# A decoder step on one core: operands and split weights of the matmuls placed at multiples of 128 bytes, moving rows and next weight rows at other parity

## The chip, the cores and the metric

The kernel runs on 1 core of one Trainium2 chip. The metric is the device time of one execution in microseconds; less is better. Engines are named as in the profile: PE is TensorE (its weight loads are listed apart as PEld), DVE is VectorE, ACT is ScalarE, POOL is GpSimd, SP is SyncE, which issues most DMA transfers.

## The reference: what is computed

One decoder layer for two sets of tokens: 512 prompt tokens and 8 x 8 sample tokens, 576 columns in all, with model width 1024. Every sub-layer is preceded by an RMS norm whose gain and shift come from a conditioning vector.

```python
x = x + 0.5 * g1 * swiglu(modulate(rms_norm(x, n1_g), sh1, sc1), w1_gate, w1_up, w1_down)
z = modulate(rms_norm(x, nm_g), sh2, sc2) @ w_in        # u, v, q, k, rv, rg, ga, gb
o_a = gelu(u) * chunk_spatial_mix(layer_norm(gelu(v)))
o_b = head_rms(retention(rotary(q), rotary(k), rv, S0)) * silu(rg)
x = x + g2 * ((sigmoid(ga) * (o_a @ w_a) + sigmoid(gb) * (o_b @ w_b)) @ w_o)
x = x + 0.5 * g3 * swiglu(modulate(rms_norm(x, n2_g), sh3, sc3), w2_gate, w2_up, w2_down)
y = rms_norm(x, final_g)
```

The feed-forward width is 2816; there are 8 retention heads. Everything is float32. Outputs are the tokens, the retention states and the normalised v rows of the samples.

## The kernel before, in words

**Split operands.** A float32 value is written as a high part, rounded to TensorE's one-pass float32 format (`F32R`), and a low part, the rest. A product of two such values takes three matmuls: high weights by high operand, high weights by low operand, low weights by high operand. ScalarE writes the high part (a copy that converts), VectorE the low part (a subtraction). Each matmul loads its own 128x128 block of weights, so the order on TensorE is load, matmul, load, matmul, and each load runs beside the matmul before it.

**Where the matmuls are.** `prod` (L648) multiplies 288 columns, half of the 576 tokens, with four blocks of 128 contraction rows, and serves both gate and up projections of the two FFNs and most of the input projection. Its moving operands are the tiles that `op` makes, filled by `Operands.hi` and `Operands.lo` (L561, L563, L568, L572 and near), and its weights come from class `Weights`: `put_hi` (L666) and `put_lo` (L674, L676). The classes `Plain` and `Pair` built on it combine four quarter products with sums of operands and of weights, so that seven products do the work of eight. `proj` (L482) multiplies 320 or 256 columns and serves the down and output projections; its weights come through `Down` and `load_w`, its moving operands are high and low tiles of 576 columns. L1350, L1363 and L1580 compute values with the roles turned: the weight matrix moves, in 256 columns, and the token tile is the stationary side. L1504 and L1515 are small products of the retention core.

**Where the tiles lie.** Tiles are rows of bytes in each of the 128 partitions. `set_in` makes a tile for split weights and starts them `INTO` = 28 elements, 112 bytes, into it. In the built program these weights start at 240, some at 112, past a multiple of 256 bytes. A moving tile of `prod` holds high parts in `[:, 0]` and low parts in `[:, 1]`, each four blocks of 288 columns; a block is 1152 bytes, nine times 128, so that blocks start in turn at 128 and at 0 past a multiple of 256. The moving tiles of `proj` start at 128 past such a multiple.

**What sets the order.** Within the three stretches `BEGIN`, `INTO_MIX` and `INTO_FFN2` a written list of steps sets the order on every engine; elsewhere it is the order of the code, with side work (conditioning products, operand splits of the mixer) put in by `tick` after each product at estimated times. Weights are fetched by SyncE's DMA queue into a ring of raw tiles, split, and used.

Of the kernel before, what the change touches and what calls it, by code (L numbers as in the profile page):

```python
# [8 lines left out]
F32 = mybir.dt.float32  # L9
F32R = mybir.dt.float32r  # L10
AF = mybir.ActivationFunctionType
ALU = mybir.AluOpType
# [3 lines left out]
P = 128  # L16
# [7 lines left out]
H = T // 2  # L24
# [10 lines left out]
FSLOT = 12  # L35
GROUPS = (5, 6, 5, 6)

INTO = 28
HALF = (slice(0, H), slice(H, T))
PART = (slice(0, 320), slice(320, T))  # L40
PW = (320, T - 320)
# [42 lines left out]
def layer_kernel(ctx: ExitStack, tc: tile.TileContext, a):  # L84
    nc = tc.nc
    PE, DVE, ACT, POOL = nc.tensor, nc.vector, nc.scalar, nc.gpsimd
# [5 lines left out]
    wp = ctx.enter_context(tc.tile_pool(name="wp", bufs=1))  # L92
# [40 lines left out]
    def nine(home, shape, dt=F32R):  # L133
        return now[home].tile(shape, dt, tag="x", name=nm(home), bufs=4 if home == "xa" else 3)

    def nine_w(shape):

        return set_in(now["xs1"], shape, 9 * 256 - shape[1] * shape[2] * shape[3], tag="x", name=nm("xw"), bufs=3)
# [4 lines left out]
    def bank():  # L143
        return pp.tile([P, 512], F32, tag="ps", name=nm("ps"), bufs=8)

    def set_in(home, shape, room=INTO, **kw):

        n = 1
        for d in shape[1:]:
            n *= d  # L150
        t = home.tile([P, n + room], F32R, **kw)[:, INTO:INTO + n]
        if len(shape) == 4:
            return t.rearrange("p (a b c) -> p a b c", b=shape[2], c=shape[3])
        return t.rearrange("p (a b c d) -> p a b c d", b=shape[2], c=shape[3], d=shape[4])
# [9 lines left out]
    def whl(shape):  # L164
        small = len(shape) == 3 and shape[1] == 1
        tag = "whs" if small else "whl"
        return set_in(
            now["whs"] if small else wp, [P] + shape, INTO if small else 64, tag=tag, name=nm(tag), bufs=1 if small else 4
        )

    def load_raw(src, k0, kc, c0, cols):
        raw = raw4([kc, cols])
        nc.sync.dma_start(
            out=raw, in_=src[k0 * P:(k0 + kc) * P, c0:c0 + cols].rearrange("(k p) c -> p k c", p=P)
        )
        return raw

    def high_low(shape):
        t = whl([2] + shape)
        return t[:, 0], t[:, 1]  # L180
# [331 lines left out]
    ops = {}  # L512

    def op(name):
        if name not in ops:
            t = nine("xs1" if name in ops["near"] else "xa", [P, 2, 4, H])
            ops[name] = t[:, 0], t[:, 1]
        return ops[name]

    class Operands:  # L520
# [20 lines left out]
        def s(self, p):  # L541
            c0, c1 = 2 * p, 2 * p + 2
            u4 = self.hb[:, c0:c1, NP:T].rearrange("p c (b l) -> p c b l", l=LS)
            s0 = self.sh * 8
            for m, op in ((self.g[:, c0:c1, 1:9], ALU.mult), (mT[:, s0 + c0:s0 + c1, 1:9], ALU.add)):
                DVE.tensor_tensor(out=u4, in0=u4, in1=m.unsqueeze(3).broadcast_to([P, 2, NB, LS]), op=op)

        def blocks(self, j):
            hb = self.hb
            return tuple(hb[:, c:c + 2, cl] for c in (2 * j, 4 + 2 * j) for cl in HALF)  # L550
# [7 lines left out]
        def hi(self, name, j):  # L558
            hi, src = op(name)[0][:, 2 * j:2 * j + 2], self.src(name, j)
            if name == "N11":  # L560
                ACT.activation(out=hi, in_=src, func=AF.Copy, scale=-1.0)  # L561
            else:
                ACT.copy(out=hi, in_=src)  # L563

        def lo(self, name, j):
            (hi, lo), src = (t[:, 2 * j:2 * j + 2] for t in op(name)), self.src(name, j)
            if name == "N11":
                DVE.scalar_tensor_tensor(  # L568
                    out=lo, in0=src, scalar=-1.0, in1=hi.bitcast(F32), op0=ALU.mult, op1=ALU.subtract
                )  # L570
            else:
                DVE.tensor_tensor(out=lo, in0=src, in1=hi.bitcast(F32), op=ALU.subtract)  # L572
# [86 lines left out]

    class Weights:  # L660
        def put_hi(self, names, src, neg=False):
            hl = whl([2, len(names), 512])
            if neg:
                ACT.activation(out=hl[:, 0], in_=src, func=AF.Copy, scale=-1.0)
            else:
                ACT.copy(out=hl[:, 0], in_=src)  # L666
            self.hl[names] = hl, src, neg

        def put_lo(self, names):
            hl, src, neg = self.hl[names]  # L670
            if neg:
                now["lo"] = DVE.scalar_tensor_tensor(
                    out=hl[:, 1], in0=src, scalar=-1.0, in1=hl[:, 0].bitcast(F32), op0=ALU.mult, op1=ALU.subtract
                )  # L674
            else:
                now["lo"] = DVE.tensor_tensor(out=hl[:, 1], in0=src, in1=hl[:, 0].bitcast(F32), op=ALU.subtract)  # L676
            for i, m in enumerate(names):
                self.w[m] = (hl[:, 0, i], hl[:, 1, i])

        def block_of(self, dst, i, z):  # L680

# [280 lines left out]
    def home_wd(c, shape):  # L962
        return set_in(now["hl"], shape, 64, tag="wd", name=nm("wd"), bufs=2)

    def home_whl(c, shape):
        return home_wd(c, shape) if c in (0, 1, 4, 5) else whl(shape[1:])
# [122 lines left out]
    for c in range(KC):  # L1089
# [11 lines left out]
        out=xall[:, :, NP:T], in_=psS[:, 0:KC * NS].rearrange("p (c t) -> p c t", c=KC))  # L1101
# [631 lines left out]
    for i in range(2):  # L1733
        for n in range(NT):
            m, z = P if n < 4 else NS, NT * i + n
# [73 lines left out]
    def home_o(c, shape):  # L1809
        if c < 2:  # L1810
            return whl(shape[1:])
        if c < 5:
            return nine_w(shape)
        return home_wd(c, shape) if c < 7 else set_in(hb_pool, shape, tag="wo", name=nm("wo"), bufs=1)

    Wo = Down(a["w_o"][0], 0, KC, home_o)
    late = []

# [6 lines left out]
    for pr in ([0], [1], [2], [3], [4], [5], [6, 7]):  # L1825
# [41 lines left out]
    hb_pool = pool(greg, "hb", "right")  # L1867
# [184 lines left out]
```

## Time and profile before

| what | value |
|---|---|
| time, 3 runs | median 1672.13 us (1667.75 to 1672.86) |
| profiled execution | 1670.48 us, its span 1668.7 us |
| TensorE matmul | busy 1637.5 us, 98% of the span, 12548 instructions |
| VectorE | busy 1154.8 us, 69% |
| ScalarE | busy 784.0 us, 47% |
| GpSimd | busy 291.5 us, 17% |
| HBM traffic | 207.01 MB read, 43.02 MB written |
| granted TensorE clock, mean | 0.996 |

A row of the page's groups reads: line, engine, operation, written tile <- read tiles, shape, count | busy us, mean ns of one | idle time ahead of it and what ended it. Matmuls are pipelined: the duration of one (some 290 ns) is longer than the distance of two starts (some 130 ns), so the pace of TensorE is read from starts, or from the chain of waits, which gives the time and the count of an unbroken run.

### The profile page before, as it was taken

Reading aid. Unit: us, or ns where it says so; the run is one execution under the profiler, and the core shown is the slowest. Engines: PE = TensorE matmul, PEld = TensorE weight load, DVE = VectorE, ACT = ScalarE, POOL = GpSimd, SP = SyncE. Lnnn points to the kernel's source line nnn. Section 1 sums busy time; section 2 is a strip of 40 time slices with the busy share of each in tenths; the row PEclk is TensorE's granted clock in tenths of the full one; section 3 lists DMA queues with packets and bytes.
Section 4 is the critical chain, followed back from the end, with each engine's and each line's share of the span. In section 5 each row is a group of like instructions: output and inputs, shape, how many; then the busy total and the mean of one; then the engine's idle time right before and its main releaser. Section 6 shows DMA issues by size and latency. Waiting matters only on the chain. (4 is left out here: it accounts for less than half of the span.)

```text
span 1668.7 us, 31368 instructions
## 1 busy us (share of the span) xinstructions
PE 1637.5 (98%) x12548; PEld 1575.7 (94%) x12548; DVE 1154.8 (69%) x1835; ACT 784.0 (47%) x1331; POOL 291.5 (17%) x372
## 2 busy tenths in 40 slices
PE   7999999999999999999999999999999999999997
PEld 4899999999999999999999999998999999999997
DVE  6867857576696877755688554677748768576773
ACT  5634524344564556644445444443237435243454
POOL 0000000000411011113346343454131000000002
PEclk9999999999999999999999999999999999999999
DMA  9553444332537776764457474798540233332321
GB/s 303 145 153 103 140 138 129 114 102 86 177 119 210 220 219 192 222 199 166 149 176 256 156 192 148 209 257 267 163 135 17 82 92 98 92 90 85 96 86 58
DMA packets 300212, 252.09 MB, mean 151 GB/s; under 512 B 13593, under 2 KB 260633, under 8 KB 300066
## 3 DMA queue, kind: packets, MB, share of 16 engines
q1 hardware_dynamic: 284594, 206.76, 41.1%
q0 software_dynamic: 13168, 40.97, 8.8%
q10 hardware_dynamic: 2304, 2.36, 0.4%
q8 instruction: 98, 1.61, 0.4%
q14 instruction: 48, 0.39, 0.1%
HBM read 207.01 MB, written 43.02 MB: 150 GB/s over the span
## 5 line engine op out<-in xcount | busy, mean ns | idle before, releaser
L648 PE MATMUL ps<-xa,whl 128*128 128x288 f32 x3000 | 423.7, 296 | 5.5 <-ACT xa L561 2.1
L648 PEld LDWEIGHTS ps<-xa,whl 128*128 128x128 f32 x3000 | 404.7, 190 | 18.2 <-issue 4.2
L648 PE MATMUL ps<-xs,whl 128*128 128x288 f32 x2040 | 289.1, 295 | 0.8 <-ACT sn L657 0.6
L648 PEld LDWEIGHTS ps<-xs,whl 128*128 128x128 f32 x2040 | 274.0, 189 | 10.9 <-issue 4.2
L676 DVE TENSOR_TENSOR whl<-wraw,whl 128x1024 fp32r<-128x1024 f32 x192 | 234.5, 1223 | 54.2 <-ACT whl L666 48.3
L666 ACT CAST whl<-wraw 128x1024 fp32r<-128x1024 f32 x192 | 200.0, 1047 | 105.8 <-DVE wraw L790 64.6
L482 PEld LDWEIGHTS ps<-c,wd 128*128 128x128 f32 x1824 | 244.2, 189 | 3.5 <-issue 3.4
L482 PE MATMUL ps<-c,wd 128*128 128x320 f32 (+1 forms) x1824 | 247.4, 296 | 0.0
L482 PE MATMUL ps<-c,whl 128*128 128x256 f32 (+1 forms) x1368 | 191.8, 298 | 1.1 <-ACT c L192 0.7
L482 PEld LDWEIGHTS ps<-c,whl 128*128 128x128 f32 x1368 | 184.3, 189 | 3.1 <-DVE c L193 0.9
L469 POOL TENSOR_TENSOR x<-x,s 128x64 f32<-128x64 f32 x72 | 35.6, 495 | 808.6 <-DVE s L468 780.7
L463 DVE SCALAR_TENSOR_TENSOR x<-ps,gate,x 128x320 f32<-128x320 f32 (+1 forms) x128 | 61.1, 481 | 120.3 <-PE ps L482 120.3
L657 ACT COPY sn<-ps 128x288 f32<-128x288 f32 x195 | 77.4, 399 | 107.5 <-PE ps L648 107.0
L185 DVE TENSOR_TENSOR whl<-wraw,whl 128x1024 fp32r<-128x1024 f32 x56 | 77.9, 1393 | 67.4 <-ACT whl L184 67.1
L949 ACT CAST wd<-wraw 128x640 fp32r<-128x640 f32 (+2 forms) x58 | 45.3, 781 | 107.7 <-PE ps L482 98.3
L1350 PE MATMUL ps<-whl,xx 128*128 128x256 f32 x768 | 88.6, 275 | 0.0
L1350 PEld LDWEIGHTS ps<-whl,xx 128*128 128x128 f32 x768 | 87.8, 188 | 0.0
L648 PE MATMUL ps<-xs,whs 128*128 128x288 f32 x480 | 69.9, 294 | 0.0
L184 ACT CAST whl<-wraw 128x1024 fp32r<-128x1024 f32 x56 | 58.5, 1048 | 22.6 <-PE ps L482 14.5
L648 PEld LDWEIGHTS ps<-xs,whs 128*128 128x128 f32 x480 | 65.7, 189 | 0.0
L666 ACT CAST whs<-wraw 128x512 fp32r<-128x512 f32 x62 | 38.5, 621 | 55.7 <-PE ps L648 46.7
L954 DVE TENSOR_TENSOR wd<-wraw,wd 128x640 fp32r<-128x640 f32 (+2 forms) x58 | 53.4, 920 | 10.1 <-ACT wd L949 9.8
(285 smaller groups left out, 2223.1 us busy)
## 6 DMA issues: line engine op xcount, KB each, us to landing
ada<-in_w_ada_dram SPq DMA_DIRECT2D x56, 512.0 KB
wraw<-in_w_in_dram SPq DMA_DIRECT2D x96, 256.0 KB
wraw<-in_w_gate_dram SPq DMA_DIRECT2D x88, 256.0 KB
wraw<-in_w_up_dram SPq DMA_DIRECT2D x88, 256.0 KB
wraw<-in_w_in_dram SPq DMA_DIRECT2D x32, 512.0 KB
wraw<-in_w_down_dram SPq DMA_DIRECT2D x32, 384.0 KB
wraw<-in_w_down_dram SPq DMA_DIRECT2D x32, 320.0 KB
accd<-c POOLq DMA_DIRECT2D x32, 288.0 KB, 5.7
```

What stands on the lines that cost most here:

```text
L184: ACT.copy(out=hi, in_=raw)
L185: now["lo"] = (eng or DVE).tensor_tensor(out=lo, in0=raw, in1=hi.bitcast(F32), op=ALU.subtract)
L463: DVE.scalar_tensor_tensor(out=x[:, o:o + w], in0=ps[:, :w], scalar=g[:, c, 0:1], in1=x[:, o:o + w], op0=ALU.mult, op1=ALU.add)
L469: return lambda: POOL.tensor_tensor(out=x[:, NP:T], in0=x[:, NP:T], in1=u, op=ALU.add)
L482: PE.matmul(ps[:, :PW[h]], lhsT=s[:, k, c0:c0 + P], rhs=m[:, PART[h]], start=k == 0 and z == 0, stop=k == kc - 1 and z == 2,)
L648: PE.matmul(ps[:, :H], lhsT=s[:, j * P:(j + 1) * P], rhs=m[:, j, :], start=fresh and j == 0 and z == 0, stop=j == 3 and z == 2, skip_group ...
L657: ACT.copy(out=t, in_=ps[:, :H])
L666: ACT.copy(out=hl[:, 0], in_=src)
L676: now["lo"] = DVE.tensor_tensor(out=hl[:, 1], in0=src, in1=hl[:, 0].bitcast(F32), op=ALU.subtract)
L949: ACT.copy(out=hl[:, 0], in_=self.raw[c])
L954: DVE.tensor_tensor(out=lo, in0=self.raw[c], in1=hi.bitcast(F32), op=ALU.subtract)
L1350: PE.matmul(ps[:, :DV], lhsT=s, rhs=m, start=i == 0, stop=i == 23)
```

## The change

All split weights and moving operands start at multiples of 128 bytes (`LINE` = 32 elements). In `Weights` the high and the low block of a weight tile are no longer adjoining: the low block starts one `LINE` further, so that the two start at other parity when addresses are counted in rows of 128 bytes; `blocks` makes such a pair. In the moving tiles of `prod` the high and low parts of one contraction block adjoin (`[P, 4, 2, H]`, low first), where before all high parts came first. So while a high operand moves, the weights that load next start in a row of the other parity, and likewise for a low operand. `home_o`'s last tile starts at its tile's beginning. No instruction is added or removed; the high and low splits write two runs of 288 columns per instruction instead of one of 576.

```diff
-INTO = 28
+LINE = 32
...
-    def set_in(home, shape, room=INTO, **kw):
+    def set_in(home, shape, room=LINE, at=LINE, **kw):
...
-        t = home.tile([P, n + room], F32R, **kw)[:, INTO:INTO + n]
+        t = home.tile([P, n + room], F32R, **kw)[:, at:at + n]
...
+    def blocks(m):
+
+        if m == 1:
+            t = now["whs"].tile([P, 2 * 512 + 2 * LINE], F32R, tag="whs", name=nm("whs"), bufs=1)[:, LINE:]
+        else:
+            t = wp.tile([P, 2 * m * 512 + 2 * LINE], F32R, tag="whl", name=nm("whl"), bufs=4)
+        return (t[:, o:o + m * 512].rearrange("p (m c) -> p m c", m=m) for o in (0, m * 512 + LINE))
...
-            t = nine("xs1" if name in ops["near"] else "xa", [P, 2, 4, H])
-            ops[name] = t[:, 0], t[:, 1]
+            t = nine("xs1" if name in ops["near"] else "xa", [P, 4, 2, H])
+            ops[name] = t[:, :, 1], t[:, :, 0]
...
         def put_hi(self, names, src, neg=False):
-            hl = whl([2, len(names), 512])
+            hi, lo = blocks(len(names))
...
-            for i, m in enumerate(names):
-                self.w[m] = (hl[:, 0, i], hl[:, 1, i])
+                self.w[m] = hi[:, i], lo[:, i]
...
-        return home_wd(c, shape) if c < 7 else set_in(hb_pool, shape, tag="wo", name=nm("wo"), bufs=1)
+        return home_wd(c, shape) if c < 7 else set_in(hb_pool, shape, at=0, tag="wo", name=nm("wo"), bufs=1)
```

More of the change, by code (lines that the diff above doesn't have):

```diff
@@ L167, in whl @@
         return set_in(
-            now["whs"] if small else wp, [P] + shape, INTO if small else 64, tag=tag, name=nm(tag), bufs=1 if small else 4
+            now["whs"] if small else wp, [P] + shape, LINE if small else 64, tag=tag, name=nm(tag), bufs=1 if small else 4
         )
+    def blocks(m):
[4 more added lines that the diff above has]
+        return (t[:, o:o + m * 512].rearrange("p (m c) -> p m c", m=m) for o in (0, m * 512 + LINE))
     def load_raw(src, k0, kc, c0, cols):
@@ L661, in put_hi @@
         def put_hi(self, names, src, neg=False):
-            hl = whl([2, len(names), 512])
+            hi, lo = blocks(len(names))
             if neg:
-                ACT.activation(out=hl[:, 0], in_=src, func=AF.Copy, scale=-1.0)
+                ACT.activation(out=hi, in_=src, func=AF.Copy, scale=-1.0)
             else:
-                ACT.copy(out=hl[:, 0], in_=src)
-            self.hl[names] = hl, src, neg
+                ACT.copy(out=hi, in_=src)
+            self.hl[names] = hi, lo, src, neg
         def put_lo(self, names):
-            hl, src, neg = self.hl[names]
+            hi, lo, src, neg = self.hl[names]
             if neg:
                 now["lo"] = DVE.scalar_tensor_tensor(
-                    out=hl[:, 1], in0=src, scalar=-1.0, in1=hl[:, 0].bitcast(F32), op0=ALU.mult, op1=ALU.subtract
+                    out=lo, in0=src, scalar=-1.0, in1=hi.bitcast(F32), op0=ALU.mult, op1=ALU.subtract
                 )
             else:
-                now["lo"] = DVE.tensor_tensor(out=hl[:, 1], in0=src, in1=hl[:, 0].bitcast(F32), op=ALU.subtract)
+                now["lo"] = DVE.tensor_tensor(out=lo, in0=src, in1=hi.bitcast(F32), op=ALU.subtract)
             for i, m in enumerate(names):
-                self.w[m] = (hl[:, 0, i], hl[:, 1, i])
+                self.w[m] = hi[:, i], lo[:, i]
         def block_of(self, dst, i, z):
```

## The prediction

> **What bounds the kernel now.** I read the busy times first, then the chain of work that ended last, then the groups of matmuls by form, then single stretches of TensorE's timeline. The two head lines of the page:
>
> ```profile
> span 1668.7 us, 31368 instructions
> PE 1637.5 (98%) x12548; PEld 1575.7 (94%) x12548; DVE 1154.8 (69%) x1835; ACT 784.0 (47%) x1331; POOL 291.5 (17%) x372
> ```
>
> TensorE works for 98% of the span and VectorE, the next, for 69%. So the time is the number of matmuls times their spacing, and what matters is whether that spacing can move. The chain (start, length, what) gives it over long unbroken runs of the two lines that issue most matmuls, L648 (the FFN and input projections) and L482 (the down and output projections):
>
> ```profile
> 1330.73 31.94 PE ps L482 x240
> 1362.67 40.99 PE ps L648 x312
> 1429.38 38.37 PE ps L482 x288
> 1467.74 29.96 PE ps L648 x228
> ```
>
> 40.99 us / 312 = 131.4 ns for a 288-column matmul of L648, and 29.96 / 228 = 131.4 again. 38.37 / 288 = 133.2 for L482, whose matmuls are half 320 and half 256 columns wide. Nothing but TensorE is in those runs. The timeline of TensorE splits the widths, and has two other lines with the same 256 columns (start, length, line, names, shape; the length of a row runs past the next start, since matmuls are pipelined, so I divide the distance of two starts by the count):
>
> ```profile
> 784.49 5.75 PE L1580 MATMUL ps<-whl,xx 128*128 128x256 f32 x48
> 790.08 0.69 PE L1504 MATMUL ps<-c,onesr 128*128 128x288 f32 x4
> ...
> 796.15 11.04 PE L1350 MATMUL ps<-whl,xx 128*128 128x256 f32 x96
> 807.03 1.98 PE L1363 MATMUL ps<-whl,hs 128*128 128x256 f32 x16
> ...
> 989.82 1.12 PE L1515 MATMUL ps<-c,c 128*128 128x256 f32 x8
> 990.78 4.79 PE L482 MATMUL ps<-c,whl 128*128 128x256 f32 x36
> ...
> 1245.39 3.67 PE L482 MATMUL ps<-xa,wo 128*128 128x320 f32 x24
> 1248.90 3.03 PE L482 MATMUL ps<-xa,xw 128*128 128x256 f32 x24
> 1251.77 0.65 PE L441 MATMUL ps<-all,onesr 128*128 128x288 f32 x2
> ```
>
> L1350: (807.03 - 796.15) / 96 = 113.3 ns. L1515: 0.96 / 8 = 120.0. L482 at 256 columns: 2.87 / 24 = 119.6, at 320 columns 3.51 / 24 = 146.3. All three load new 128x128 weights for each matmul and none waits, yet L1350 is 6 to 7 ns faster on the same shape. The widths of L482 give the price of a column, (146.3 - 119.6) / 64 = 0.417 ns, so L1350's spacing carried to the other widths is 113.3 + 32 x 0.417 = 126.7 ns at 288 and 140.0 at 320. L648 stands 4.7 ns above that, L482 6.3 at each width. The groups by form say the same in durations:
>
> ```profile
> L648 PE MATMUL ps<-xa,whl 128*128 128x288 f32 x3000 | 423.7, 296 | 5.5 <-ACT xa L561 2.1 <-ACT whl L666 1.4 <-DVE whl L676 1.3
> L482 PE MATMUL ps<-c,wd 128*128 128x320 f32 x912 | 143.8, 310 | 0.0
> L482 PE MATMUL ps<-c,wd 128*128 128x256 f32 x912 | 118.9, 283 | 0.0
> L1350 PE MATMUL ps<-whl,xx 128*128 128x256 f32 x768 | 88.6, 275 | 0.0
> L1515 PE MATMUL ps<-c,c 128*128 128x256 f32 x64 | 9.2, 282 | 0.0
> ```
>
> 275 ns in L1350 against 283 in L482 at one width.
>
> **What differs between the fast and the slow lines.** Only where the operands lie. Take the byte distance, modulo 256, from the start of a moving operand to the start of the weights that load beside it (the next matmul's), as the built program places them. L1350, L1363 and L1580: 144, the weights starting on a multiple of 128. L1515: 0, both on multiples of 128. L482: 112, the weights 16 bytes short of such a multiple. L648: 112 or 240, changing with every contraction block, since a block's columns are nine rows of 128 bytes. So 144 costs 113.3 ns; 0 and 112 cost about 120; 112 and 240 in turn cost 131.4 where 126.7 would match. In the changed program the distance is 128 on 5,727 of 5,744 successive pairs of L648, 3,966 of 3,987 of L482, and all of L1350; that the edit fails to do what it says is no rival.
>
> **The change, part by part.** It adds and removes no instruction, and the order on all five engines is row for row the same.
>
> *Spacing of L648.* The distance becomes 128, which the trace never holds for a stretch. Bounds: from the row at 144 (126.7 ns) to the row at 0, 120.0 + 32 x 0.417 = 133.3. I take 126.7. Parity alone does not part fast from slow (112 is other parity for most of the bytes and slow), alignment of the weights alone does not either (0 is aligned and slow); 144 has both, and 128 has both. There are 3000 + 2040 + 480 + 264 = 5784 such matmuls by their groups:
>
> ```profile
> L648 PE MATMUL ps<-xs,whl 128*128 128x288 f32 x2040 | 289.1, 295 | 0.8 <-ACT sn L657 0.6
> L648 PE MATMUL ps<-xs,whs 128*128 128x288 f32 x480 | 69.9, 294 | 0.0
> L648 PE MATMUL ps<-xa,whs 128*128 128x288 f32 x264 | 38.8, 295 | 0.0
> ```
>
> 5784 x 4.7 = 27.2 us saved; by the other bound 5784 x 1.9 = 11.0 lost.
>
> *Spacing of L482.* The groups of the line, with shortest, median and longest duration in ns:
>
> ```profile
> L482 PE MATMUL ps<-c,wd x1824: 277/307/495, 110.5 to 1651.5; 128*128 128x320 f32 x100, 128*128 128x256 f32 x83
> L482 PE MATMUL ps<-c,whl x1368: 276/306/500, 417.8 to 1657.7; 128*128 128x320 f32 x98, 128*128 128x256 f32 x98
> L482 PE MATMUL ps<-xx,whl x384: 276/307/500, 909.4 to 1044.7; 128*128 128x320 f32 x96, 128*128 128x256 f32 x96
> ```
>
> With five smaller ones that is 4032. From 133.2 to (113.3 + 140.0) / 2 = 126.7: 4032 x 6.5 = 26.2 us saved; by the other bound nothing, as it already pays the 120.
>
> *L1350, L1363, L1580.*
>
> ```profile
> L1580 PE MATMUL ps<-whl,xx 128*128 128x256 f32 x384 | 46.9, 279 | 0.0
> L1363 PE MATMUL ps<-whl,hs 128*128 128x256 f32 x128 | 15.8, 275 | 0.0
> L1580 PE MATMUL ps<-whl,hs 128*128 128x256 f32 x64 | 8.2, 280 | 0.0
> ```
>
> With L1350's 768 these are 1344 matmuls, and they go from 144 to 128. The bounds are 0 and (120.0 - 113.3) x 1344 = 9.0 us lost; by the same choice as above I take 0.
>
> *What is given back.* A run does not reach its pace at once: L1580's 48 after a break need (790.08 - 784.49) / 48 = 116.5 ns instead of 113.3, 0.15 us more in all, a part of it the break itself. The faster runs will be broken by the conditioning products, which come in groups of 8 and of 4, 28 + 18 times by these rows, and by the attention core's:
>
> ```profile
> L304 PE MATMUL ps<-ada,cs 128*32 128x512 f32 x224 | 31.7, 605 | 0.0
> L316 PE MATMUL ps<-ident,ada 128*128 128x128 f32 x72 | 11.0, 275 | 4.5 <-ACT ada L310 4.5
> ```
>
> I take 60 breaks x 0.1 = 6 us, an estimate. Then other engines must keep pace:
>
> ```profile
> 1362.51:1403.50 40.99, 40.99 (x315) 40.99 (x314) 32.84 (x50) 21.29 (x35) 0.32 (x1) 1.00 0.28 80
> 1100.00:1140.00 40.00, 38.97 (x321) 36.60 (x319) 26.01 (x41) 18.61 (x40) 21.65 (x22) 1.00 0.91 239
> ```
>
> ```profile
> DMA  9553444332537776764457474798540233332321
> ```
>
> (Stretch, its length, then busy PE, PEld, DVE, ACT, POOL, the clock, DMA share, GB/s; and the page's DMA share in 40 slices, in tenths.) In the FFN, VectorE has 32.84 of 40.99 us; TensorE at 126.7 would need 39.5, so it stays covered. Near 1100 us the DMA engines are busy 0.91 of the time and TensorE already pauses. Three slices of 41.7 us (7, 9, 8) carry such traffic, 125 us, of which L482's gain of a twentieth, 6 us, is at stake; I take half, 3.
>
> *Operand splits in two pieces.* With high and low halves interleaved by block, the 84 copies and subtractions that write operands (7 names, two halves each, high and low, three phases) write two runs of 288 instead of one of 576.
>
> ```profile
> L588 DVE TENSOR_TENSOR hb<-hb 128x576 f32<-128x576 f32 x16 | 12.0, 752 | 1.0 <-ACT hb L537 0.9
> L193 DVE TENSOR_TENSOR c<-c,c 128x576 fp32r<-128x576 f32 x32 | 27.2, 867 | 15.2 <-ACT c L192 15.0
> ```
>
> L588 already reads and writes two runs per row and takes 752 ns, L193 writes one and takes 867, so I price the second run at 0. The bounds are what one such row could differ, 115 ns either way, times 84 = 10 us, almost all behind TensorE; without that cover only the first splits of each phase count, under 1 us. The same goes for the weight splits of L666 and L676, which only start elsewhere.
>
> *A moved wait.* The weights' small buffer grows by 144 bytes, tiles behind it shift, and one wait on a GpSimd store moves from one state load to the one queued before it on SyncE, and likewise between two updates of L1519 on VectorE. The queue passes the same wait one entry sooner; I put it at 0, bounded by one update, 0.7 us:
>
> ```profile
> L1519 DVE SCALAR_TENSOR_TENSOR S<-S,ps 128x512 f32<-128x512 f32 x32 | 19.9, 680 | 3.4 <-PE ps L1515 3.4
> ```
>
> Sum: -27.2 - 26.2 + 0 + 6 + 3 = -44.4 us. The profiled execution took 1670.48 us for its span of 1668.7, so 1.8 lie around it; it is 1.65 below the median of 1672.13. 1670.5 - 44.4 = **1626 us**.
>
> **A rule against it.** The Trainium skill, page "TensorE: Matmul & The Clock Gate", section "Step-by-step: what each phase is for", says that the moving operand and the weight load have separate read ports of SBUF, so that loading the next weights takes nothing from the running matmul. By that the distance could not matter and the sum would be 0. The rows at 113.3 and 119.6 ns speak against it, though not finally, since the lines differ in their tiles too.
>
> **Rivals.**
>
> *No change.* Spacing differs for a reason that goes with the tiles (which pool, how far apart in memory), not with the distance modulo 256: 1670 us. For it: 112 and 0 cost the same although they lie far apart. Against it: L482 is slow with weights out of four kinds of tile (wd, whl, xw, wo).
>
> *Slower, by a window.* What counts is by how far the weight rows trail the moving rows, and the good window lies above 128 bytes and holds 144 only. Then L648 goes to 133.3 (+11.0 us), L482 stays, and L1350 and its like lose their pace (+9.0): 1670.5 + 20 = 1690 us. 128 lies midway between 112, slow, and 144, fast; the case decides if the edge is past 128.
>
> *The wrong neighbour.* A weight load lasts longer than the spacing, by its shortest, median and longest duration:
>
> ```profile
> L648 PEld LDWEIGHTS ps<-xa,whl x3000: 186/188/334, 35.9 to 1615.9; 128*128 128x128 f32 x188
> ```
>
> 188 ns against 131: if it still reads when its own matmul begins, that matmul is disturbed by its own weights, and the change puts two of the three products (high by low, low by high) at distance 0 from them. L648 then stands at (126.7 + 2 x 133.3) / 3 = 131.1, 0.3 ns under now, and L482, by the same mean of its two widths, at 131.1 against 133.2: 1.7 + 8.5 = 10 us saved, 1660 us. Against it: a part of the 188 ns must be delay between issue and reading, since in L1350 loads of the same length follow each other every 113.3 ns.
>
> *Half.* The pace is reached only in one of the two lines, or after long runs: 8 to 35 us saved, about 1648 us.
>
> **How the numbers follow.** Forecast 0.55, half or wrong neighbour 0.14, no change 0.11, the window 0.20. The range goes from 1612 (every saving and nothing given back, 1617, less 5, the spread of the three runs) to 1680, which takes in no change and part of the window's case; the forecast's own range is 1612 to 1641. A measurement of this kernel tells 0.3%, 5 us, from no change. Faster by more: 0.55 + 0.14 - 0.02 = 0.67; within: 0.13; slower: 0.20.
>
> **What will show it.** Right: the L648 group's mean near 290 (its shortest is 289) and the chain's run of 312 in about 39.6 us; L482 near 275 to 277 ns at 256 columns and 302 at 320; L1350 still 275; VectorE's and ScalarE's busy times as now. Wrong: L1350 at 282, the window; L648 unchanged with L482 faster, the wrong neighbour; all three unchanged, the rule of separate ports; TensorE faster but idle in between, a cover of mine that failed.

## The result, and the profile after

The changed kernel takes 1683.11 us (median of 4 runs, 1681.49 to 1685.25) against 1670.49 us for the kernel before (median of 4, 1667.75 to 1672.86): 1.0077 times as long, 95% interval 1.0054 to 1.0100. That is 0.8% slower, clear of the noise. The forecast was 1626 us.

The head of the changed kernel's page:

```profile
span 1679.7 us, 31367 instructions
PE 1652.1 (98%) x12548; PEld 1589.5 (95%) x12548; DVE 1154.8 (69%) x1835; ACT 785.4 (47%) x1331; POOL 287.1 (17%) x372
```

The span grew by 11.0 us. TensorE's busy time grew by more, 1652.1 - 1637.5 = 14.6 us, and its idle time shrank from 31.2 to 27.6 us (span less busy). The other engines are nearly as busy as they were: VectorE 1154.8 us in both, ScalarE 785.4 after 784.0, GpSimd 287.1 after 291.5. The change therefore lies in the spacing of matmuls. The chain of waits shows it on unbroken runs (start, length, what; lines stand 8 further down than before, so L648 is now L656, L482 is L490, L1350 is L1358):

```profile
1372.28 67.36 PE ps L656 x504
1439.64 38.19 PE ps L490 x288
1477.82 56.18 PE ps L656 x420
```

L656: 67.36 / 504 = 133.7 ns and 56.18 / 420 = 133.8, where it was 131.4. L490: 38.19 / 288 = 132.6, where it was 133.2. TensorE's timeline gives each width by the distance of starts:

```profile
802.23 11.55 PE L1358 MATMUL ps<-whl,xx 128*128 128x256 f32 x96
813.62 1.59 PE L1371 MATMUL ps<-whl,hs 128*128 128x256 f32 x12
...
1254.50 3.68 PE L490 MATMUL ps<-xa,wo 128*128 128x320 f32 x24
1258.02 3.00 PE L490 MATMUL ps<-xa,xw 128*128 128x256 f32 x24
1260.86 0.65 PE L449 MATMUL ps<-all,onesr 128*128 128x288 f32 x2
...
1372.12 1.76 PE L656 MATMUL ps<-xs,whl 128*128 128x288 f32 x12
...
1378.52 4.96 PE L656 MATMUL ps<-xa,whl 128*128 128x288 f32 x36
```

L1358: 11.39 / 96 = 118.6 ns, where it was 113.3. L490: 3.52 / 24 = 146.7 at 320 columns (was 146.3) and 2.84 / 24 = 118.3 at 256 (was 119.6). L656: 48 matmuls start between the last two rows, 6.40 / 48 = 133.3. The mean over all unbroken starts of the line says the same, 133.3 after 131.3; the chain's 133.7 and 133.8 are a little higher. The groups by form agree: 282 ns of duration in L1358 where 275 stood, 297 in L656 where 296 stood, 282 in L490 at 256 columns where 283 stood.

```profile
L656 PE MATMUL ps<-xa,whl 128*128 128x288 f32 x3000 | 427.9, 297 | 5.5 <-ACT xa L569 2.2 <-ACT whl L674 1.4 <-DVE whl L684 1.3
L490 PE MATMUL ps<-c,wd 128*128 128x256 f32 x912 | 118.3, 282 | 0.0
L1358 PE MATMUL ps<-whl,xx 128*128 128x256 f32 x768 | 92.7, 282 | 0.0
```

With the counts of the prediction: L656 5784 x 1.9 = +11.0 us, L1358 and its like 1344 x 5.3 = +7.1, L490 4032 x -0.6 = -2.4. The sum, +15.7, stands beside the 14.6 us by which TensorE's busy time grew; its idle time shrank by 3.6 us, which leaves the 11.0 of the span.

What was left to find out: is it the distance itself that sets these paces, which of the change's two parts does it, and was there any placement that would have given the 126.7 ns.

### The profile page after: what moved, and what is told of

It reads as the page before. It is cut to its first block, busy times and chain, and to the rows that moved or that the text cites. A ratio compares the mean times of both kernels' runs of the same rounds, so it can differ in the third digit from the quotient of the medians.

```text
span 1679.7 us, 31367 instructions
## 1 busy us (share of the span) xinstructions
PE 1652.1 (98%) x12548; PEld 1589.5 (95%) x12548; DVE 1154.8 (69%) x1835; ACT 785.4 (47%) x1331; POOL 287.1 (17%) x372
## 5 line engine op out<-in xcount | busy, mean ns | idle before, releaser
L656 PE MATMUL ps<-xa,whl 128*128 128x288 f32 x3000 | 427.9, 297 | 5.5 <-ACT xa L569 2.2
L656 PEld LDWEIGHTS ps<-xa,whl 128*128 128x128 f32 x3000 | 408.9, 188 | 18.0 <-issue 5.0
L656 PE MATMUL ps<-xs,whl 128*128 128x288 f32 x2040 | 293.0, 296 | 0.0
L656 PEld LDWEIGHTS ps<-xs,whl 128*128 128x128 f32 x2040 | 278.2, 188 | 9.5 <-issue 4.2
L490 PE MATMUL ps<-c,wd 128*128 128x320 f32 (+1 forms) x1824 | 246.5, 296 | 0.0
L490 PEld LDWEIGHTS ps<-c,wd 128*128 128x128 f32 x1824 | 243.2, 188 | 3.5 <-issue 3.4
L490 PE MATMUL ps<-c,whl 128*128 128x256 f32 (+1 forms) x1368 | 191.0, 297 | 1.1 <-ACT c L200 0.7
L490 PEld LDWEIGHTS ps<-c,whl 128*128 128x128 f32 x1368 | 183.4, 188 | 3.2 <-DVE c L201 0.9
L1358 PE MATMUL ps<-whl,xx 128*128 128x256 f32 x768 | 92.7, 282 | 0.0
L1358 PEld LDWEIGHTS ps<-whl,xx 128*128 128x128 f32 x768 | 91.8, 188 | 0.0
L656 PE MATMUL ps<-xs,whs 128*128 128x288 f32 x480 | 70.6, 295 | 0.0
L656 PEld LDWEIGHTS ps<-xs,whs 128*128 128x128 f32 x480 | 66.3, 188 | 0.0
```

The source lines that it names most:

```text
L490: PE.matmul(ps[:, :PW[h]], lhsT=s[:, k, c0:c0 + P], rhs=m[:, PART[h]], start=k == 0 and z == 0, stop=k == kc - 1 and z == 2,)
L656: PE.matmul(ps[:, :H], lhsT=s[:, j * P:(j + 1) * P], rhs=m[:, j, :], start=fresh and j == 0 and z == 0, stop=j == 3 and z == 2, skip_group ...
L1358: PE.matmul(ps[:, :DV], lhsT=s, rhs=m, start=i == 0, stop=i == 23)
```

## The experiments

In what follows a pace is the mean time from the start of one matmul to the start of the next, and the distance is that of the prediction: bytes, modulo 256, from the start of a moving operand to the start of the weights that load beside it. The theory of the prediction was that distance with alignment decides and 128 is a good one; its main rivals were a window (only distances near 144 are good), separate read ports (distance decides nothing), and a weight load that disturbs its own matmul.

### e1_sweep: streams of matmuls at 16 distances

A kernel of streams alone: 96 matmuls in a row, each with new weights, no other engine at work beside them; one stream follows the other without a pause. Series w shifts the weights, series m the moving operand, and series a alternates both by 128 bytes, so that the next weights lie at the stated distance while a matmul's own weights lie 128 bytes off it.

```diff
+for k in range(COUNT):
+    w, m = w0 + k % 8 * 192, m0 + k % 4 * 576
+    if side == "a":
+        w, m = w + (k + 1) % 2 * 32, m + k % 2 * 32
+    PE.matmul(ps[:, :width], lhsT=big[:, w:w + P], rhs=big[:, m:m + width], ...)
```

> The spacing measured by itself: nothing of the decoder is computed; one tile of rounded random numbers is used as weights and as moving operand in streams of 96 matmuls, 256, 288 and 320 columns wide, every matmul with new weights. The byte distance from a moving operand to the weights loaded beside it, modulo 256, goes from 0 to 240 in steps of 16, three times: w, moving operands on multiples of 128 and weights off them; m, weights on multiples of 128 and moving operands off them; a, moving operands in turn on even and odd rows of 128 bytes and the weights too, so that the next weights keep the distance and a matmul's own weights have it plus 128. Window theory (the next weights' distance counts, and 128 lies outside a window that holds 144): at 256 columns about 113.3 ns at 144 and 118.7 to 120 at 0, 112 and 128, w and m alike, a like w. Alignment theory (weights must start on a multiple of 128): 113.3 for m at 144, about 120 for w at 144. Own-weights theory: the curve a is the curve w moved by 128, so a at 16 is as fast as w at 144. Tile theory (the distance is not the cause): one spacing for all, at 256 columns near 113 or near 119.

TensorE's timeline (the tile's name has the width, the distance and the series):

```profile
112.89 11.55 PE L46 MATMUL n256d128w<-big 128*128 128x256 f32 x96
124.27 11.52 PE L46 MATMUL n256d144w<-big 128*128 128x256 f32 x96
135.63 11.67 PE L46 MATMUL n256d160w<-big 128*128 128x256 f32 x96
...
305.30 11.10 PE L46 MATMUL n256d144m<-big 128*128 128x256 f32 x96
316.24 11.68 PE L46 MATMUL n256d160m<-big 128*128 128x256 f32 x96
...
666.79 12.96 PE L46 MATMUL n288d128w<-big 128*128 128x288 f32 x96
679.58 12.76 PE L46 MATMUL n288d144w<-big 128*128 128x288 f32 x96
```

At distance 128 a plain stream needs 11.38 / 96 = 118.5 ns at 256 columns and 12.79 / 96 = 133.2 at 288; at 320 it needs 146.7. Those are the changed kernel's three paces, with no other engine at work. So nothing else in the decoder is needed to make them, and the rule of separate ports as the prediction had used it ("the distance could not matter") falls: the same 256-column stream runs at 113.4 ns (w at 64), at 118.5 (128) and at 120.0 (160).

But the prediction's picture falls with it. At 144, 256 columns, 118.3 ns with the weights shifted (11.36 / 96) and 114.0 with the moving operand shifted (10.94 / 96): one distance, two paces. In m 112 is fast too (113.3), in w it is slow (119.9); 64 is fast in both. So neither alignment, nor parity, nor a window of distances orders them. Series a moves between 116.6 and 119.9 and doesn't repeat w shifted by 128, so a load that disturbs its own matmul doesn't order them either. Each of these figures is one stream behind one other stream; e10 shows how far that limits them. And no stream of 288 columns came below 130.0 (a, 80 and 240), nor one of 320 below 143.4 (a, 176): the 126.7 and 140.0 of the forecast didn't show up.

### e2_pattern: the kernel's own orders

The same, with the three products in the kernel's order (high by high, low moving operand, low weights). Each series is a pattern of 128-byte shifts: a is the order of L648 before (operand blocks alternate, low parts at the same parity as the high ones), g that of the changed kernel (blocks don't alternate, low operand and low weights 128 bytes further), e has both the alternation and the low shifts, f neither.

```diff
+j, z = k // 3, k % 3
+w = w0 + j % 4 * 320 + (1600 + 32 * low_w if z == 2 else 0)
+m = m0 + j % 4 * 320 + (j % 2 * 32 if flip else 0) + (1600 + 32 * low_x if z == 1 else 0)
```

> Nothing of the decoder is computed. Streams of 96 matmuls in the order of the decoder's products (high by high, high by low, low by high, next block), with the start of the weights moved in steps of 16 bytes. Series: a has the moving rows of the kernel before at 288 columns (blocks in turn at 0 and 128, high and low alike), b to e the same with low weights, low operands or both 128 bytes further; f has constant moving rows, as L482; g is the changed kernel's order, low operand and low weights each 128 further. If spacing is set by offsets alone, a at 112 gives L648's 131.3 ns of before, g at 128 gives the 133.3 of after, f at 112 gives 119.5 to 120 and 146.7, f at 128 gives 118.7 and 146.7. If only the next weights' distance counts, g equals the plain stream of the run before at every distance; if own weights count too, it differs. If something else in the decoder sets the pace (other engines, DMA), a at 112 and g at 128 do not repeat its numbers.

```profile
110.95 12.76 PE L49 MATMUL n288awd112x<-big 128*128 128x288 f32 x96
123.55 12.96 PE L49 MATMUL n288awd128x<-big 128*128 128x288 f32 x96
...
1040.03 12.76 PE L49 MATMUL n288gwd0x<-big 128*128 128x288 f32 x96
1052.63 13.06 PE L49 MATMUL n288gwd16x<-big 128*128 128x288 f32 x96
...
1141.93 12.97 PE L49 MATMUL n288gwd128x<-big 128*128 128x288 f32 x96
1154.74 12.94 PE L49 MATMUL n288gwd144x<-big 128*128 128x288 f32 x96
```

a at 112, the kernel before: 12.60 / 96 = 131.3 ns, and L648 had 131.4. g at 128, the changed kernel: 12.81 / 96 = 133.4, and L656 has 133.3. The stream reproduces both kernels. For `proj`, f at 112 gives 119.9 ns at 256 columns and at 128 it gives 118.6, where the mean of L482 was 119.4 and that of L490 is 118.6. g at 0, the change's rule reversed (moving rows and next weight rows at the same parity), gives 131.3, better than at 128; e at 0 gives 130.2 over the 96 matmuls and 130.0 over the last 24. At 320 columns series f stays at 146.7 almost everywhere.

### e3_into32: the alignment alone

The kernel before, with its split weights started at a multiple of 128 bytes and no other change.

```diff
-INTO = 28
+INTO = 32
```

> The kernel before with its weights at 32 elements instead of 28, nothing else: alignment alone, without the parity part. Distances: L482 and L1350, L1363, L1580 go to 128, L648 to 0 and 128 in turn. By the curves of the plain streams: L1350's group 113.4 to 118.7 ns per matmul, so 1344 x 5.3 = +7 us; L482 119.4 and 147.0 to 118.7 and 146.7, -2 us; L648 near the mean of 131.8 and 133.3, 132.6 against 131.3, +7 us: 1682 us, as slow as the whole change. If it was the parity part (two-run operands, other tile layout) that cost the time, this one stays near 1670.

Measured 1681.03 us (1679.65 to 1685.40, 4 runs), 1.0071 times before (1.0056 to 1.0087). The chain of waits has L648, still in the old arrangement of blocks, at 67.24 / 504 = 133.4 ns:

```profile
1370.55 67.24 PE ps L648 x504
```

L1350 stands at 118.9 ns. The shift of the weights by 16 bytes alone brings the whole loss; the intervals of this kernel and of the changed one overlap, so the parity part on top of it neither saves nor costs anything that these runs can tell.

### e4_after_v28: the values' weights back at their old place

The changed kernel, with only the products of L1358, L1371 and L1588 back at distance 144: their moving side is a weight tile from `load_w`, which begins 112 bytes into its tile again.

```diff
-    def whl(shape):
+    def whl(shape, at=LINE):
...
-        return [load_w(win, 4 * kk, 4, V0 + i * 512 + z * 256, 256) for kk in range(2)]
+        return [load_w(win, 4 * kk, 4, V0 + i * 512 + z * 256, 256, LINE - 4) for kk in range(2)]
```

> The changed kernel with one part undone: the weights that move in L1350, L1363 and L1580 start at 28 elements again, so their distance is 144 as before. Distance theory: these lines return from 118.7 to 113.4 ns, 1344 x 5.3 = 7 us less than the changed kernel, about 1676, with L648 still at 133.3. If L1350 is slow for another reason than its own distance (what runs before it, other tiles), it stays at 118.7 and the time at 1683.

Measured 1677.28 us (1675.82 to 1678.88, 4 runs), ratio to before 1.0045 (1.0031 to 1.0058). By the group's duration and the starts the pace of the line is back (276 ns, 113.8 ns apart), and the 5.8 us gained stand against 1344 x 5.3 = 7.1:

```profile
L1358 PE MATMUL ps<-whl,xx 128*128 128x256 f32 x768 | 88.9, 276 | 0.0
```

So that term of the sum is real and is nearly half of the loss.

### e5_far64: `proj` at distance 64

The streams had one distance that was fast from both sides, 64 at 256 columns. The kernel before, with only L482's weights moved there (`load_w`'s and `Down`'s begin 16 elements into their tile; the weights of `prod` and of the values keep their 28).

```diff
-    def set_in(home, shape, room=INTO, **kw):
+    def set_in(home, shape, room=INTO, at=16, **kw):
...
-            hl = whl([2, len(names), 512])
+            hl = whl([2, len(names), 512], INTO)
```

> The kernel before with only L482's weights moved, from distance 112 to 64. The plain stream at 64 gave 113.3 ns at 256 columns and 146.7 at 320. Distance theory: L482 at 256 columns from 119.4 to 113.3, 2016 x 6.1 = 12 us less than the kernel before, 1658 us (ratio 0.993), at 320 columns no change, L648 and L1350 untouched. If offsets act through the aligned rows only (128 bytes), 64 is nothing special and the time stays at 1670.

Measured 1663.22 us (1662.42 to 1664.05, 5 runs), 0.9958 times before (0.9945 to 0.9972): 6.5 us below the kernel before, where about 12 were expected, and below the changed one too. Chain and group:

```profile
1326.80 31.21 PE ps L482 x240
```

```profile
L482 PE MATMUL ps<-c,wd 128*128 128x256 f32 x912 | 114.7, 278 | 0.0
```

The chain's run of 240 is at 31.21 / 240 = 130.0 ns, where in the kernel before it had 31.94 / 240 = 133.1. But over the kernel the 256-column matmuls mean 115.3 ns, not 113.3 (278 ns of duration, between 275 and 283): some groups of them go at 113.3 and others, at the same distance, at 117.7 to 118. At 320 columns nothing changed (146.6).

### e6_loads: what of it is the weight load, what the moving operand

Streams at six distances: a, b, c, e load weights of 32, 64, 96 and 128 columns; in r the moving operand is one row of 128 bytes over and over, in z a single element with stride 0.

```diff
+if how == "r":
+    rhs = big[:, m:m + 32].unsqueeze(1).broadcast_to([P, width // 32, 32])
+if how == "z":
+    rhs = big[:, m:m + 1].broadcast_to([P, width])
+PE.matmul(out, lhsT=big[:, w:w + cols], rhs=rhs, ...)
```

> Nothing of the decoder is computed. The plain stream at distances 0, 64, 112, 128, 144 and 240, with shorter loads and with other moving reads: a, b, c load weights of 32, 64 and 96 columns, e of 128; r moves one and the same 128-byte row over and over, z one and the same element. If the excess comes from reads of the load and of the moving operand meeting in SBUF, it must shrink with the load's length (32 columns: 256-column spacing at every distance at or under the 113.3 of the best one) and z, which reads hardly anything, must lie at or under the best spacing whatever the distance. If it comes from the order of loads and matmuls inside TensorE, z and e show the same numbers and the distance means nothing to z.

```profile
44.26 11.04 PE L50 MATMUL n256ad112x<-big 128*32 128x256 f32 x96
55.14 11.04 PE L50 MATMUL n256ad128x<-big 128*32 128x256 f32 x96
...
221.96 11.68 PE L50 MATMUL n256ed0x<-big 128*128 128x256 f32 x96
233.48 11.06 PE L50 MATMUL n256ed64x<-big 128*128 128x256 f32 x96
244.37 11.68 PE L50 MATMUL n256ed112x<-big 128*128 128x256 f32 x96
...
804.06 11.92 PE L50 MATMUL n288zd0x<-big 128*128 128x288 f32 x96
815.82 11.92 PE L50 MATMUL n288zd64x<-big 128*128 128x288 f32 x96
...
888.39 14.24 PE L50 MATMUL n320ad64x<-big 128*32 128x320 f32 x96
902.46 14.24 PE L50 MATMUL n320ad112x<-big 128*32 128x320 f32 x96
```

With the moving element standing still the distance means nothing: 111.7, 122.5 (11.76 / 96) and 135.8 ns at 256, 288 and 320 columns at every distance. So what lies above that is bound to the reading of the moving rows: at 288 columns the kernel before pays 131.4 and the changed one 133.3. With loads of 32 columns, 256 columns run at 113.3 to 113.5 ns at five of the six distances (10.88 / 96 at 112, where full loads need 119.9; the sixth, at 0, was the first stream of all and went at 117.8 over its last 24), so at this width the slow paces come from load and moving read together. The length doesn't order them simply: at 144 loads of 64 columns go at 120.0, of 96 at 116.7. At 288 columns short loads go at 130.0 to 131.7, full ones at 131.2 to 133.3. At 320 columns short loads stay at 146.6 (14.07 / 96), as long ones do, at five distances, so there it is not the load's length; at distance 0 they go at 143.4. The row over and over (r) was no faster than moving rows: 120.0, 133.3 to 136.6, 146.7 to 153.1.

The Trainium skill, page "TensorE: Matmul & The Clock Gate", section "Back-to-back issue gap", gives N / 2.4 + 2.5 ns as the warm gap of an isolated matmul of N columns, with nothing in it for the load of weights; the estimate by it is 109.2 at 256, 122.5 at 288 and 135.8 at 320. The runs with the moving element standing still agree at 288 and 320 and lie 2.5 ns above it at 256. With contiguous rows of this float format they don't agree: no stream of 288 or 320 columns with full loads came nearer than 7.5 ns.

### e7_fine: is there a distance at which 288 columns go at 126.7?

All 64 distances in steps of 4 bytes; at 288 columns eight series (orders a, c, e, g, h, i with the weights shifted, a and g with the moving operand shifted), at 256 and 320 the plain one from both sides; 48 matmuls each.

```diff
-COUNT = 96
+COUNT = 48
...
-    for dist in range(0, 256, 16):
+    for dist in range(0, 256, 4):
```

> Nothing of the decoder is computed. Streams in the decoder's orders, the start moved in steps of 4 bytes over 256: 288 columns in series a, c, e, g, h, i (weights moved) and a, g (moving operands moved), 256 and 320 columns in series f. If what I carried over in the prediction holds, that the best pace of 256 columns exists at other widths too, some offset gives 126.7 at 288 and 140.0 at 320. If the 16-byte steps of the runs before already show all there is, nothing lies below 130.0 at 288 columns and 144.4 at 320, and the prediction's gain was not to be had at any offset.

```profile
1041.55 6.41 PE L49 MATMUL n288ewd128x<-big 128*128 128x288 f32 x48
1047.79 6.51 PE L49 MATMUL n288ewd132x<-big 128*128 128x288 f32 x48
...
4336.67 7.05 PE L49 MATMUL n320fwd180x<-big 128*128 128x320 f32 x48
4343.56 7.20 PE L49 MATMUL n320fwd184x<-big 128*128 128x320 f32 x48
```

The lowest of 512 streams at 288 columns is 6.24 / 48 = 130.0 ns; the lowest of the plain ones at 320 is 143.5 (6.89 / 48), usually 146.7. At 256 columns six streams of 128 came within 1 ns of 113.3. Of the gain that the forecast counted on, 4.7 ns on each L648 matmul, at most 1.4 exist at these placements, and on L482's 320 columns at most 3 of 6.3.

### e8_after_swap: the change's rule reversed

The changed kernel with high and low weight blocks exchanged, so that the moving rows of L656 and the next weight rows lie at the same parity (distance 0), everything else as changed.

```diff
-            hi, lo = blocks(len(names))
+            lo, hi = blocks(len(names))
```

> The changed kernel with one thing reversed: high and low weight blocks change places, so that in L648 the next weights always start in a row of the same parity as the moving operand (distance 0 in place of 128). If other parity is the better one and something else spoiled the change, this is slower than the changed kernel. By the streams in the decoder's order (series g: 133.3 ns at 128, 131.1 at 0) it is faster: L648 from 133.3 to 131.1, 5784 x 2.2 = 12.7 us less than the changed kernel, about 1670, with L482 and L1350 as in the changed kernel (118.6 and 118.7 at 256 columns).

Measured 1673.32 us (1670.67 to 1676.77, 9 runs), ratio to before 1.0019 (1.0009 to 1.0029). The chain has L656 at 29.91 / 228 = 131.2 ns, as series g at 0 did:

```profile
1471.08 29.91 PE ps L656 x228
```

So "other parity" is not what a placement should seek here: with the same parity the kernel is about 10 us faster than with the other, which is 5784 x 1.9 = 11.0 within the spread of the runs. It is still some 3 us slower than the kernel before, as L1358 keeps its 118.9 ns (7 us) and L490 its small gain (2).

### e9_both: distance 64 for `proj`, series e for `prod`

e5 with L648's operands and weights laid out as series e at distance 0, 130.0 ns in the stream. The operand's eight blocks stand as low, high, high, low for each pair of contraction blocks, the weights come from `blocks` as in the change.

```diff
-            t = nine("xs1" if name in ops["near"] else "xa", [P, 2, 4, H])
-            ops[name] = t[:, 0], t[:, 1]
+            t = nine("xs1" if name in ops["near"] else "xa", [P, 8, H])
+            ops[name] = Halves(t, 1), Halves(t, 0)
```

> A version meant to beat both: the kernel before with L482's weights at distance 64 (1663 us by the run before), L1350's as before, and L648 in the order of series e (high and low operands at other parity, blocks in turn, high and low weights at other parity), whose stream took 130.0 ns against 131.1 for the order of the kernel before. By the streams 5784 x 1.1 = 6 us less than 1663: 1657 us, ratio 0.992 to the kernel before; L648 at 130.0 to 130.3, L482 at 115.3 and 146.6, L1350 at 113.8. If the runs between breaks (12 to 24 matmuls in the decoder's products) are too short to settle in that pace, L648 stays at 131 to 132 and the time at 1663 or above.

Measured 1665.52 us (1662.44 to 1666.68, 7 runs), 0.9967 times before (0.9954 to 0.9980): faster than the kernel before, and not told apart from e5, whose interval overlaps. The 1657 us that had been expected didn't come. The chain shows where it was lost (here L648 is L666):

```profile
1359.79 41.28 PE ps L666 x312
...
1464.77 29.66 PE ps L666 x228
```

One run of this layout goes at 41.28 / 312 = 132.3 ns, the other at 29.66 / 228 = 130.1, and the mean of the line is 131.6, no better than the 131.4 of the kernel before. As in e5, one placement has two paces. `proj` shows it too: its runs of 240, laid out as in e5, take 31.20 and 31.73 us here (130.0 and 132.2 ns), where e5 had 31.21 both times.

### e10_starts: does the pace depend on what ran before?

Streams of 48 matmuls, five placements, each behind 24 matmuls of one of eight streams; the whole twice over, without a pause.

```diff
+for turn in "uv":
+    for t in TARGETS:
+        for p in AHEAD:
+            stream(f"{n}from{w}{k}d{d}{turn}", 24, *p)
+            ps = stream(f"{n}after{w}{k}d{d}{turn}", 48, *t)
```

> Nothing of the decoder is computed. Five streams of 48 matmuls at fixed offsets (256 columns at 64 and at 144 with weights moved, 288 columns in the orders of the version before at 112, of the changed kernel at 128, and of series e at 0), each run right after 24 matmuls of eight other kinds, and all of it twice. If a pace belongs to the offsets alone, a stream's last 24 spacings are the same after all eight. If the state left by the run ahead counts, one and the same stream settles at more than one pace, the same one in both repeats: 113.3 or 117.7 to 118.3 at 64, as L482 did in the kernel with distance 64 (115.3 on average), 130.0 or 132 to 133 in series e, as L648 did in the last kernel (131.6). The spread over starts then says how far a long stream's pace may be carried over to short runs.

In the names, "after" is the stream measured and what it follows:

```profile
51.10 5.82 PE L48 MATMUL n256fd64after256fd128u<-big 128*128 128x256 f32 x48
56.75 3.32 PE L48 MATMUL n256fd64from288ad112u<-big 128*128 128x288 f32 x24
59.91 5.62 PE L48 MATMUL n256fd64after288ad112u<-big 128*128 128x256 f32 x48
65.37 3.35 PE L48 MATMUL n256fd64from288ad0u<-big 128*128 128x288 f32 x24
...
157.54 5.76 PE L48 MATMUL n256fd144after320fd180u<-big 128*128 128x256 f32 x48
163.14 3.69 PE L48 MATMUL n288ed0from320fd112u<-big 128*128 128x320 f32 x24
...
185.62 6.41 PE L48 MATMUL n288ed0after256fd0u<-big 128*128 128x288 f32 x48
191.87 3.04 PE L48 MATMUL n288ed0from256fd128u<-big 128*128 128x256 f32 x24
194.75 6.51 PE L48 MATMUL n288ed0after256fd128u<-big 128*128 128x288 f32 x48
201.11 3.31 PE L48 MATMUL n288ed0from288ad112u<-big 128*128 128x288 f32 x24
```

It does. 256 columns at distance 64: 5.65 / 48 = 117.7 ns behind 256 columns at 128, and 5.46 / 48 = 113.8 behind 288 columns in series a. 288 columns in series e at 0: 130.2 ns behind 256 columns at 0, 6.36 / 48 = 132.5 behind 256 columns at 128. 256 columns at 144, weights shifted, have three paces: 119.6 to 120.0 ns behind six of the eight, 118.3 behind series a at 0, and 5.60 / 48 = 116.7 behind 320 columns at 180. The second turn repeats the first. Two placements hardly cared: series a at 112 (131.0 to 131.7 behind the eight) and g at 128 (132.9 to 133.3). These two are the kernel before and the changed one, which fits that both of those have one steady pace for their main line. That e5 and e9 got only a part of what their streams had shown fits it too, but inside the kernel no run separates what ran ahead.

This also limits e1 and e7, where each stream had one fixed stream ahead of it. The reading "one distance, two paces" stands: at 144 with the weights shifted the plain streams with full loads lie, over e1, e2, e6, e7 and e10, between 116.7 and 120.0 ns, with the moving operand shifted between 113.8 and 114.0 in e1, e2 and e7. But m at 112 had 113.3 in e1 and 116.8 in e7, and m at 128 had 118.7 and 120.1, so a difference of 1 to 4 ns between two single streams isn't shown to be the placement's own.

## Why the prediction was wrong

**The step that failed first: 126.7 ns for distance 128.** The prediction gave bounds from the row at 144 (126.7) to the row at 0 (133.3) and took the first, because "144 has both, and 128 has both", alignment and other parity. Measured: 133.3, the other bound. The argument had a few lines of one kernel, at a few distances, and looked for the one property that parted them; e1 shows that distances don't part into fast and slow at all (144 is 118.3 or 114.0 at 256 columns, by which side is shifted), and alignment doesn't either (at 64 with the weights off a multiple of 128 it is 113.4, at 128 with them on one 118.5). Nor is the place "only" what can differ between a fast and a slow line: in e10 one placement moved by 3.3 ns with what ran ahead. With the other bound in every term its own sum was 1670.5 + 11.0 + 9.0 = 1690 us. The measured paces come to 15.7 for that sum's 20, because L1358 went to 118.6 and not to 120.0 and L490 fell by 0.6.

**The step that failed second: the 126.7 itself.** L1350's 113.3 ns at 256 columns was carried to 288 and 320 by L482's price of a column, 0.417 ns. That price came from slow rows, and slow rows do lie on one line: 120.0, 133.3 and 146.7 ns are each 13.3 above 0.417 times their columns. The fast ones don't: the lowest paces found with full loads, 113.3, 130.0 and 143.4, lie 6.6, 10.0 and 10.1 above it. So of the 53 us of saving, 27.2 and 26.2, all but the part of L482's 256 columns, 2016 x 6.3 = 12.7 us, rested on two paces that no stream reached, and none of the placements tried shows the paces that the forecast time needs.

**L482.** Priced at -26.2 with the bound "nothing". It was nearly the bound: 132.6 for 133.2, -2.4 us. (Its own rows give 6.3 ns at both widths, not 6.5, which would have made 25.4; next to the miss this is nothing.)

**L1350, L1363, L1580.** Priced at 0 with a bound of 9.0 lost: 7.1 by the starts, 5.8 by e4.

**What is given back, +6 and +3.** There was no faster run to be broken and no faster demand on DMA, so no run here shows these terms. The 3.6 us by which TensorE's idle time shrank fit the picture that a slower TensorE hides more of its waits, but no run separates it.

**Splits in two pieces and the moved wait.** Priced at 0, and nothing speaks against it: VectorE's busy time is the same to the tenth, ScalarE's differs by 1.4 us.

**The rivals.** "Slower, by a window" had the right sign and nearly the right prices, and its sign of being right came (282 ns in L1358), but by luck: there is no window, as 64, and 112 and 144 with the moving operand shifted, are fast in e1 while 80 and 128 between them are slow. "Wrong neighbour" expected L656 unchanged; it rose by 1.9 ns, and series a in e1 speaks against it. "No change", because the pace goes with the tiles: e3, e4 and e5 moved only starts within the same kinds of tile, and the paces moved with them. "Half" didn't occur, as neither line gained more than 0.6 ns. The rule against the forecast: the Trainium skill, "TensorE: Matmul & The Clock Gate", section "Step-by-step: what each phase is for", says that loading the next weights takes no read bandwidth from the running matmul. These runs show that the pace does hang on where the two lie (113.3 against 120.0 ns) and, at 256 columns, on how many columns the load has, so for this format and shape the measurement decides against what the prediction drew from it, that the distance could not matter.

**What stays open.** That the excess is bound to reading moving rows is shown by z, and that the load has a part in it at 256 columns by the short loads. What makes some placements settle at one pace whatever ran before and others at one of two or three, and what at 320 columns keeps most short loads at 146.6, isn't settled by these runs.

## What to carry to other kernels

A pace that differs between two lines of a profile is a reason to measure placements in a bare stream of the kernel's own order, not to derive a rule from three points: g at 128 in the stream gives the changed kernel's 133.4 ns without the kernel, and measured ahead of the rewrite it would have told of the loss. Carry a price only across rows of the same kind, and treat the best row at one width as evidence for that width alone. And where a steady stream has more than one pace, its fastest is not what a kernel gets: of the 12 us that the stream of distance 64 promised 6.5 came (e5), and of the 5784 x 1.4 = 8 us that series e promised beyond them none (e9). So the stream should have the kernel's own neighbours ahead of it.

## What the runs showed of the hardware that wasn't expected

- Back-to-back float matmuls with new 128x128 weights each have paces of 113.3 to 120.0 ns at 256 columns, 130.0 to 133.3 at 288 and 143.4 to 146.7 at 320 for most placements, at a granted clock of 1.00 and with no other engine at work (in e7 the rest go up to 122.9, 137.8 and 153.1, the three streams of the third point aside); with a moving operand of stride 0 they have 111.7, 122.5 and 135.8 at each of six distances.
- One placement can have two or three steady paces, chosen by what ran before and kept over 48 matmuls: 113.8 and 117.7 ns, 130.2 and 132.5, and 116.7, 118.3 and 120.0 (e10).
- Three of the 256-column streams of e7 (weights at 28, 32 and 36 bytes) went at 133.3 ns, the pace of 288 columns, between neighbours at 122.1 and 119.0; at 32 bytes e1 had 118.3. The granted clock was 1.00 there, and the three ran one right behind the other; whether what ran ahead made this pace isn't shown.
- The fastest version measured is not the change but e5, the weights of L482 moved by 48 bytes: 1663.22 us, 6.5 below the kernel before and 19.9 below the changed one.
